# A first modulation in five uneven pieces with its x and value weights loaded piece by piece, and a last 512-column projection done as two halves

## The chip, the cores and the metric

The kernel runs on one core of one Trainium2 chip. The metric is the device time of one execution in microseconds (us); less is better. The kernel before was run three times: 1462.21, 1459.61 and 1459.7 us, median 1459.7 us.

## The reference, cut to what matters

One inference step of two layers (DEPTH = 2) over 384 tokens of width 1024: 128 prompt tokens and 256 sample tokens. Each layer has a mixing part and a feed-forward part (FFN), and each part starts from a modulated input. All data is float32.

```
ada   = silu(c) @ ada_w + ada_b              c: one row for the prompt, one for the sample
shift, scale, ... = split(ada)               each of 1024 columns
h     = x * (1 + scale) + shift              the modulated input (h1 for the mixing part)
mix   = mLSTM(h @ in_w[...]) , conv(...) , retention(h @ in_w[...]) , joined by gates
x     = layer_norm(alpha * x + gate * mix)
h2    = x * (1 + scale2) + shift2
x     = layer_norm(alpha * x + gate2 * (silu(h2 @ w1) * (h2 @ w3)) @ w2)
```

The change touches two places: the first modulation of the first layer with the two value projections that consume it (h @ in_w for the mLSTM values and for the retention values, 512 columns each), and the very last product of the second layer's FFN with its layer norm.

## The kernel before, in words

**Tiles and number format.** The 384 tokens are three token tiles of 128 (t = 0 the prompt, t = 1 and 2 the sample). The width of 1024 is eight feature tiles of 128. A float32 product is made of three matmuls on parts that are rounded to a shorter format: `split` (lines 208 to 210) takes a high part of a weight (`whi`, a cast on ScalarE, line 209) and the rest (`wlo`, a subtraction on VectorE, line 210), and `accum` (lines 255 to 261) issues high by high, high by low, low by high (lines 259, 260, 261). Weights arrive by DMA in tiles `wraw` of 1 MB (three buffers).

**Who sets the order.** A tile scheduler orders each engine's instructions from the program text, dependences and buffers; on an engine they then run in that order. Loads are issued by SyncE (SP) in one queue, strictly in order. A DMA is given one of eight completion semaphores in turn, so an issue also waits until the DMA eight places before it has landed.

**The head, lines 976 to 1074.** x is loaded whole, three DMAs of 512 KB (lines 997, 999), and TensorE turns all of it into feature-major tiles `xT` by 24 transposes (line 1005). The first modulation then goes in four pieces q of two feature tiles each. `ada_load(q)` loads the 2 MB of `ada_w` that give shift and scale for those 256 columns, as four DMAs with rows of 256 numbers (line 988), and two small DMAs of `ada_b` (line 994). `ada_part` multiplies them with silu(c) (16 matmuls of 32x256 in the program, each two in the trace, `adaps`, line 1021) and adds the bias on VectorE (line 1024). `ada_mod` spreads the result over partitions (`modps`, line 1030), copies it (lines 1031, 1032), applies it to `xT` on ScalarE (`hfs`, line 1037) and splits h into `h1h` and `h1l` (VectorE, lines 1039, 1040). Six accumulations `vacc` (two value projections by three token tiles, each one bank of PSUM of 512 columns) take the feature tiles of a piece as they come: 144 matmuls of 512 columns in all. The value weights come as four `wraw` tiles of 1 MB, two in front of piece 1's `ada_w` and two in front of piece 3's (line 215, `load_v`). The table `AORD` says after which accumulation the `ada_part` and `ada_mod` of the next piece stand.

**What follows the head.** On SP: constants (`cc`, line 1077), states and small vectors (lines 1081 to 524), the gate weights `wg` (line 812, 64 KB in very short rows), vectors `vr` (lines 1095, 1098), and then the first two 1 MB tiles of the mixing weights (line 247), called r0 and r1 here: r0 holds feature tiles 0 to 3, r1 feature tiles 4 to 7 of the same 512 output columns. On TensorE: the gate product (line 818, 16 matmuls), then the mixing products (lines 259 to 261, `ps`, 384 columns), which use r0 first and r1 after it, with one gate transposition between (line 542).

**The tail.** `proj` (from line 462) runs the last product: per half hf of 512 output columns and per token tile t, `tokB` accumulates 8 feature tiles per 1024 rows of w2, and `resid` (line 426) scales (line 429, `gmix`), adds to x (line 433) and takes statistics (line 437, `bn`). For hf = 1 `norm` follows: line 442 joins the statistics, line 324 and GpSimd's line 325 make the reciprocal root, lines 450 and 451 apply it to two halves of x, and `put_out` (line 491 to 493) stores them.

## Time and profile before

| | |
|---|---|
| median of three runs | 1459.7 us |
| the profiled execution's own time | 1460.56 us |
| its span in the trace | 1458.8 us |
| TensorE (PE) matmul busy | 1424.8 us, 98% of the span |
| VectorE (DVE) busy | 927.9 us, 64% |
| ScalarE (ACT) busy | 589.0 us, 40% |
| GpSimd (POOL) busy | 64.6 us, 4% |
| moved by DMA | 226.08 MB, 155 GB/s over the span |
| mean granted TensorE clock | 0.993 of full speed |

Times in the trace start at 0 with the span. The timeline view has one row for a run of equal instructions: start, how long the run took from its first start to its last end, engine, line, operation, what is written from what, shapes and count, and in brackets how long the engine was idle before it and what ended that. The profiled execution is 0.86 us above the median of the runs; 1.8 us of its time lie outside the span.

### The profile page before, as it was taken

The page shows a single profiled execution, that of the slowest core. Times are in us where ns is not written, and L with a number is a line of the kernel's source. Part 1 is how long each engine was busy: PE and PEld are TensorE (multiplying, and loading weights), DVE is VectorE, ACT ScalarE, POOL GpSimd, SP SyncE. Part 2 cuts the span into 40 slices and gives each one's busy share as a digit, 9 for nine tenths or more (in the row PEclk, how much of TensorE's full clock was granted, in tenths as well). Part 3 has the DMA queues.
Part 4 walks back from the last instruction along what each step waited for, and adds up shares of the span by engine and source line. Part 5 has one row for each costly group of instructions (what it writes and reads, how often), then busy time and mean ns, then how long its engine had stood idle before and what let it go on. Part 6 is the DMA issues. An engine that isn't in the chain of part 4 may idle for free.

```text
span 1458.8 us, 20429 instructions
## 1 busy us (share of the span) xinstructions
PE 1424.8 (98%) x7990; PEld 1295.3 (89%) x7990; DVE 927.9 (64%) x1845; ACT 589.0 (40%) x1090; POOL 64.6 (4%) x102
## 2 busy tenths in 40 slices
PE   6999999999999999999999999899999999999997
PEld 4799999989988888979977999899999889898996
DVE  3455798987747545354374559879886666544447
ACT  3445458423525323323334365544335254242430
POOL 1000002000100000000000000110000000000000
PEclk8999999999999999999999999999999999999999
DMA  9565255465374474645655332342535526243441
GB/s 316 178 233 177 95 138 172 145 223 182 117 260 159 149 255 138 223 153 177 211 152 162 130 120 66 84 123 88 164 99 170 173 73 203 89 158 100 145 159 43
DMA packets 131712, 226.08 MB, mean 155 GB/s; under 512 B 12552, under 2 KB 62200, under 8 KB 126496
## 3 DMA queue, kind: packets, MB, share of 16 engines
q1 hardware_dynamic: 130144, 222.65, 47.0%
q0 software_dynamic: 1472, 2.14, 0.5%
q8 instruction: 62, 1.02, 0.3%
q14 instruction: 34, 0.28, 0.1%
HBM read 221.05 MB, written 3.71 MB: 154 GB/s over the span
## 4 chain that ended last, share of the span: by engine, by line
PE 83%; DMA 7%; DVE 6%; ACT 2%; issue 1%; POOL 0%; SPq 0%; DVEq 0%; POOLq 0%; ACTq 0%
PE ps L259 25%; PE ps L261 24%; PE ps L260 24%; DMA wraw<-in_in_w_dram 4%; PE adaps L377 3%; DMA adaq<-in_ada_w_dram 1%; DVE wlo L210 1%; DMA wada<-in_ada_w_dram 1%; DVE cacc L783 1%; PE vacc L259 1%; PE vacc L261 1%; PE vacc L260 1%; ACT whi L209 1%; PE adaps L1021 0%; DVE dl L636 0%
## 5 line engine op out<-in xcount | busy, mean ns | idle before, releaser
L209 ACT CAST whi<-wraw 128x512 fp32r<-128x512 f32 (+1 forms) x484 | 337.5, 723 | 593.8 <-PE ps L260 248.3
L210 DVE TENSOR_TENSOR wlo<-wraw,whi 128x512 fp32r<-128x512 f32 (+1 forms) x484 | 383.5, 813 | 215.3 <-PE ps L261 104.1
L259 PE MATMUL ps<-h1h,whi 128*128 128x384 f32 x896 | 306.9, 343 | 3.2 <-ACT whi L209 1.7
L261 PE MATMUL ps<-h1h,wlo 128*128 128x384 f32 x896 | 300.9, 336 | 1.1 <-DVE wlo L210 1.0
L260 PE MATMUL ps<-h1l,whi 128*128 128x384 f32 x896 | 300.2, 335 | 0.0
L259 PE MATMUL ps<-h2h,whi 128*128 128x384 f32 x576 | 193.9, 337 | 0.0
L261 PE MATMUL ps<-h2h,wlo 128*128 128x384 f32 x576 | 192.6, 334 | 0.0
L260 PE MATMUL ps<-h2l,whi 128*128 128x384 f32 x576 | 192.6, 334 | 0.0
L259 PEld LDWEIGHTS ps<-h1h,whi 128*128 128x128 f32 x896 | 168.9, 189 | 18.2 <-ACT whi L209 7.0
L261 PEld LDWEIGHTS ps<-h1h,wlo 128*128 128x128 f32 x896 | 168.6, 188 | 2.2 <-DVE wlo L210 2.0
L260 PEld LDWEIGHTS ps<-h1l,whi 128*128 128x128 f32 x896 | 169.0, 189 | 0.1
L783 DVE SCALAR_TENSOR_TENSOR cacc<-u,cwt,cacc 128x399 f32<-128x399 f32 x232 | 144.3, 627 | 1.9
L259 PEld LDWEIGHTS ps<-h2h,whi 128*128 128x128 f32 x576 | 108.1, 188 | 8.5 <-issue 5.0
L260 PEld LDWEIGHTS ps<-h2l,whi 128*128 128x128 f32 x576 | 108.1, 188 | 0.2
L261 PEld LDWEIGHTS ps<-h2h,wlo 128*128 128x128 f32 x576 | 108.1, 188 | 0.0
L259 PE MATMUL ps<-whi,fAh 128*128 128x512 f32 x264 | 103.4, 392 | 0.0
L261 PE MATMUL ps<-whi,fAl 128*128 128x512 f32 x264 | 102.9, 390 | 0.0
L260 PE MATMUL ps<-wlo,fAh 128*128 128x512 f32 x264 | 102.8, 389 | 0.0
L429 DVE TENSOR_TENSOR gmix<-ps,lnc 128x512 f32<-128x512 f32 x48 | 33.1, 689 | 84.8 <-PE ps L261 84.8
L963 DVE TENSOR_TENSOR gf<-ps,sig 128x384 f32<-128x384 f32 x36 | 20.1, 557 | 84.7 <-PE ps L261 84.7
L259 PEld LDWEIGHTS ps<-whi,fAh 128*128 128x128 f32 x264 | 49.6, 188 | 14.1 <-issue 4.2
L261 PEld LDWEIGHTS ps<-whi,fAl 128*128 128x128 f32 x264 | 49.6, 188 | 10.4
(307 smaller groups left out, 1997.5 us busy)
## 6 DMA issues: line engine op xcount, KB each, us to landing
wraw<-in_in_w_dram SPq DMA_DIRECT2D x64, 1024.0 KB
wada<-in_ada_w_dram SPq DMA_DIRECT2D x40, 1024.0 KB
wraw<-in_ffn_w_dram SPq DMA_DIRECT2D x76, 512.0 KB
wraw<-in_ffn_w_dram SPq DMA_DIRECT2D x28, 1024.0 KB
wraw<-in_out_w_dram SPq DMA_DIRECT2D x8, 1024.0 KB
adaq<-in_ada_w_dram SPq DMA_DIRECT2D x8, 512.0 KB
wraw<-in_mlstm_out_w_dram SPq DMA_DIRECT2D x4, 1024.0 KB
wraw<-in_ret_out_w_dram SPq DMA_DIRECT2D x4, 1024.0 KB
```

Source lines behind the costliest of these rows:

```text
L209: nc.scalar.copy(hi, src)
L210: tt(lo, src, hi.bitcast(F32), op=ALU.subtract)
L259: mm(out, sh, vh, start=(first and i == 0), stop=False)
L260: mm(out, sh, vl, start=False, stop=False)
L261: mm(out, sl, vh, start=False, stop=(last and i == n - 1))
L377: mm(st["ps"][32 * g:32 * g + 32, :], cs[:, k, :], wt[:, 512 * g:512 * g + 512], start=(k == 0), stop=(k == KT - 1))
L429: tt(g, ps, lc[0 if t == 0 else 1, hf], op=ALU.mult)
L783: tc.keep_in_program_order(stt(ac, u[:, k:k + CW], wk, ac, op0=ALU.mult, op1=ALU.add))
L963: tt(f, ps, sg[j], op=ALU.mult)
```

## The change

**Head.** The first modulation goes in five pieces of 1, 2, 2, 2 and 1 feature tiles (`PIECES`). A piece of one tile loads 1 MB of `ada_w` in rows of 128 numbers (512 B) into another buffer, in two DMAs; a piece of two tiles loads as before. x comes in columns: the first 128 columns of the three token tiles through ScalarE's queue, then 256, 256 and 384 columns through SP's, each in front of the piece that needs them, and the transposes are issued one feature tile at a time (`x_turn`) from the table `todo` between the accumulations. The first 512 rows of the two value weights come in three steps each (feature tile 0, tiles 1 and 2, tile 3), the second 512 rows as 1 MB each, and they are split per feature tile (128x512) and not per two (128x1024).

**Tail.** In the last product of the kernel, the last token tile's second 512 columns are accumulated as two halves of 256 columns, one after the other, each with its own `resid`; the statistics of that token tile are taken in groups of 256.

```diff
-AORD = {(0, 0): ((1, 1, 0, 16),), (0, 1): ((0, 1),), (0, 4): ((1, 2, 0, 16),), (0, 5): ((0, 2),),
-        (1, 3): ((1, 3, 0, 16),), (1, 5): ((0, 3),)}
+PIECES = ((0, 1), (1, 2), (3, 2), (5, 2), (7, 1))
...
     def resid(t, hf, ps, lc, first, stats, c=slice(0, 512)):
...
+            if t not in bns:
+                bns[t] = [tmp((P, 4, 6), f"bn{t}", 1), 0]
+            for c0 in range(s.start, s.stop, stats):
+                nc.vector.bn_stats(bns[t][0][:, bns[t][1], :], x[t][:, c0:c0 + stats])
+                bns[t][1] += 1
...
-                ps = tokB(src, wl, t)
+                parts = [slice(0, 512)]
+                stats = 512 if final else 0
+                if final and after is None and t == NT - 1:
+                    stats = 256
+                    if hf == 1:
+                        parts = [slice(0, 256), slice(256, 512)]
+                for c in parts:
+                    ps = tokB(src, [(h[:, c], l_[:, c]) for h, l_ in wl], t)
+                    with urgent() if final and hf == 1 else nullcontext():
+                        resid(t, hf, ps, lc, first, stats, c)
...
+    def load_v(h, k0, k1, which=(0, 1)):
+        for i in which:
+            off = (O_MV, O_RV)[i]
+            if k0 == 0:
+                raws[h, i] = wp.tile([P, 4, 512], F32, tag="wraw", name="wraw", bufs=WRAW)
+            r0 = h * 512 + k0 * P
+            nc.sync.dma_start(raws[h, i][:, k0:k1, :],
+                              inw[r0:r0 + (k1 - k0) * P, off:off + 512].rearrange("(k p) f -> p k f", p=P))
...
+    x_load(nc.scalar, slice(0, P))
+    ada_load(0)
+    xT = []
+    x_turn(0)
+    load_v(0, 0, 1)
+    x_load(nc.sync, slice(P, 3 * P))
+    ada_part(0)
     ada_mod(0)
...
+    ada_load(1)
+    load_v(0, 1, 3)
+    x_load(nc.sync, slice(3 * P, 5 * P))
+    todo = {0: [(1, x_turn, 1), (1, x_turn, 2), (3, ada_part, 1), (4, ada_mod, 1)],
+            1: [(1, x_turn, 3), (1, x_turn, 4), (3, ada_part, 2), (4, ada_mod, 2), (4, v_pre, 3)],
+            2: [(0, x_turn, 5), (0, x_turn, 6), (2, ada_part, 3), (3, ada_mod, 3), (4, x_turn, 7)],
+            3: [(2, ada_part, 4), (3, ada_mod, 4)]}
+    for pi, (f0, nf) in enumerate(PIECES):
+        if pi == 0:
+            ada_load(2)
+            load_v(0, 3, 4)
+            x_load(nc.sync, slice(5 * P, D))
+        elif pi == 1:
+            load_v(1, 0, 4, (0,))
+            ada_load(3)
+        elif pi == 2:
+            load_v(1, 0, 4, (1,))
+            ada_load(4)
...
```

**Where instructions move: SP, the first loads.** Before (x, the first piece, the first value weights, the second piece):

```order
L186 DMA cc<-consts_dram 128x130
L997 DMA x_77<-in_x_prompt_dram 128x1024
L999 DMA x_78<-in_x_sample_dram 128x1024
L999 DMA x_79<-in_x_sample_dram 128x1024
L988 DMA adaq<-in_ada_w_dram 128x6x256
L988 DMA adaq<-in_ada_w_dram 128x2x256
L988 DMA adaq<-in_ada_w_dram 128x4x256 x2
L994 DMA adaq<-in_ada_b_dram 2x256 x2
L215 DMA wraw<-in_in_w_dram 128x4x512 x2
L988 DMA adaq<-in_ada_w_dram 128x6x256
```

Now, from the same first row to the first DMA of the second piece (the first 128 columns of x are on ScalarE's queue and not in these rows):

```order
L185 DMA cc<-consts_dram 128x130
L1013 DMA adaq<-in_ada_w_dram 128x8x128 x2
L1018 DMA mrows<-in_ada_b_dram 2x128 x2
L1071 DMA wraw<-in_in_w_dram 128x512 x2
L990 DMA x_77<-in_x_prompt_dram 128x256
L992 DMA x_78<-in_x_sample_dram 128x256
L992 DMA x_79<-in_x_sample_dram 128x256
L1071 DMA wraw<-in_in_w_dram 128x2x512
L1013 DMA adaq<-in_ada_w_dram 128x6x256
```

The 1 MB of piece 0 now stands in front of everything but the small constants, and less of x and of the value weights stands in front of piece 1. From the constants that follow the last piece on (line 1077 before, 1134 now) SP's rows are the same.

**TensorE, the first mixing products.** Before, from the gate transposition on (`h1h_96` is feature tiles 0 to 3 and so needs r0; `h1h_98` is tiles 4 to 7 and needs r1); twelve matmuls on r0 stand in front of these rows:

```order
L542 MATMUL ps_668<-cc_75,mgT_622 128x16 x3
L259 MATMUL ps_715<-h1h_96,whi_636 128x384
L260 MATMUL ps_715<-h1l_97,whi_636 128x384
L261 MATMUL ps_715<-h1h_96,wlo_637 128x384
L259 MATMUL ps_715<-h1h_96,whi_636 128x384
L259 MATMUL ps_642<-h1h_98,whi_630 128x384
L260 MATMUL ps_642<-h1l_99,whi_630 128x384
```

Now, the last rows ahead of the first one on r1; here thirteen matmuls on r0 and the gate transposition stand in front of the first row:

```order
L260 MATMUL ps_696<-h1h_96,wlo_685 128x384
L260 MATMUL ps_769<-h1h_96,wlo_691 128x384
L258 MATMUL ps_769<-h1h_96,whi_690 128x384
L259 MATMUL ps_769<-h1l_97,whi_690 128x384
L260 MATMUL ps_769<-h1h_96,wlo_691 128x384
L258 MATMUL ps_696<-h1h_98,whi_684 128x384
L259 MATMUL ps_696<-h1l_99,whi_684 128x384
```

The first matmul that needs r1 is the 17th of the mixing products before and the 19th now.

**VectorE, the last token tile.** Before, from the last normalising instruction of t = 1 (`x_78`) on:

```order
L451 SCALAR_TENSOR_TENSOR x_78<-x_78,rs,lnc 128x512 x2
L429 TENSOR_TENSOR gmix<-ps,lnc 128x512
L433 TENSOR_TENSOR x_79<-x_79,gmix 128x512
L437 BN_STATS bn_12944<-x_79 128x6
L442 BN_AGGR mv<-bn_12944 128x2
```

Now:

```order
L453 SCALAR_TENSOR_TENSOR x_78<-x_78,rs,lnc 128x512 x2
L428 TENSOR_TENSOR gmix<-ps,lnc 128x256
L432 TENSOR_TENSOR x_79<-x_79,gmix 128x256
L428 TENSOR_TENSOR gmix<-ps,lnc 128x256
L437 BN_STATS bn_12998<-x_79 128x6
L432 TENSOR_TENSOR x_79<-x_79,gmix 128x256
L437 BN_STATS bn_12998<-x_79 128x6
L444 BN_AGGR mv<-bn_12998 128x2
```

Both halves of the last token tile (`x_79`) stand behind the whole chain of t = 1; three instructions of 512 columns became six of 256.

## Rows read from the trace of the kernel before

**Rows 1.** The page: TensorE's busy time.

```profile
PE 1424.8 (98%) x7990; PEld 1295.3 (89%) x7990; DVE 927.9 (64%) x1845; ACT 589.0 (40%) x1090; POOL 64.6 (4%) x102
```

**Rows 2.** Windows of 10 us: busy per engine, granted clock, DMA share, GB/s.

```profile
10.00:20.00 10.00, 5.34 (x52) 3.51 (x50) 4.08 (x11) 4.07 (x9) 0.52 (x1) 0.91 0.94 348
20.00:30.00 10.00, 8.41 (x44) 4.59 (x44) 5.26 (x5) 3.45 (x4) 0.00 (x0) 0.57 1.05 374
50.00:60.00 10.00, 10.00 (x58) 7.22 (x57) 2.88 (x10) 3.57 (x8) 0.00 (x0) 1.00 0.09 10
```

**Rows 3.** Chain of waits up to 80 us: start, us, what.

```profile
3.90 7.54 DMA adaq<-in_ada_w_dram
11.46 13.39 DMA adaq<-in_ada_w_dram
```

**Rows 4.** Timeline of the head, TensorE.

```profile
14.84 0.64 PE L1021 MATMUL adaps<-adaq,cs 128*32 128x256 f32 x8 [0.68 <-DMA adaq<-in_ada_w_dram]
...
20.56 0.80 PE L259 MATMUL vacc<-whi,h1h 128*128 128x512 f32 x1 [3.15 <-DVE h1l L1040]
...
24.89 1.93 PE L1021 MATMUL adaps<-adaq,cs 128*32 128x256 f32 x16 [0.57 <-DMA adaq<-in_ada_w_dram]
...
29.15 1.07 PE L1021 MATMUL adaps<-adaq,cs 128*32 128x256 f32 x16
```

**Rows 5.** Timeline, TensorE: prices of the head's operations.

```profile
7.06 4.95 PE L1005 MATMUL ps<-cc,x 128*128 128x128 f32 x24 [7.06 <-DMA x<-in_x_prompt_dram]
...
36.29 1.93 PE L1021 MATMUL adaps<-adaq,cs 128*32 128x256 f32 x32
...
39.65 0.95 PE L1030 MATMUL modps<-cc,adaq 128*128 128x2 f32 x8
...
66.14 0.39 PE L259 MATMUL vacc<-whi,h1h 128*128 128x512 f32 x1
...
68.86 0.34 PE L818 MATMUL ps<-h1h,wgr 128*32 128x384 f32 x1
```

**Rows 6.** SP's timeline behind the last piece.

```profile
47.26 1.63 SPq L520 DMA_DIRECT2D m0b<-in_state_mlstm_m_dram  x1
...
58.73 0.27 SPq L1095 DMA_DIRECT2D vr<-in_ln_w_dram  x1
...
71.50 0.27 SPq L1095 DMA_DIRECT2D vr<-in_ln_w_dram  x1
```

**Rows 7.** SP's waits up to 100 us: waited for, us in total, times, longest.

```profile
SPq L1095 <- DMA wg<-in_in_w_dram: 6.1, 1, 6.1
SPq L1095 <- DMA wraw<-in_in_w_dram: 6.0, 2, 4.1
```

**Rows 8.** Timeline, the first mixing products and a cast of their weights.

```profile
69.55 1.15 ACT L209 CAST whi<-wraw 128x512 fp32r<-128x512 f32 x2
...
71.66 0.33 PE L259 MATMUL ps<-h1h,whi 128*128 128x384 f32 x1
...
75.23 0.51 PE L259 MATMUL ps<-h1h,whi 128*128 128x384 f32 x2
```

**Rows 9.** DMA view of 22.8 to 28.2 us.

```profile
DMA packets 2099, 2.08 MB, mean 386 GB/s; under 512 B 66, under 2 KB 2099, under 8 KB 2099
```

**Rows 10.** DMA view of 47.2 to 48 us.

```profile
DMA packets 557, 0.17 MB, mean 208 GB/s; under 512 B 452, under 2 KB 541, under 8 KB 556
```

**Rows 11.** Timeline of the tail.

```profile
1449.00 1.41 DVE L451 SCALAR_TENSOR_TENSOR x<-x,rs,lnc 128x512 f32<-128x512 f32 x2
...
1450.20 0.39 PE L261 MATMUL ps<-whi,fAl 128*128 128x512 f32 x1
1450.62 0.69 DVE L429 TENSOR_TENSOR gmix<-ps,lnc 128x512 f32<-128x512 f32 x1 [0.21 <-PE ps L261]
...
1452.80 0.21 DVE L442 BATCH_NORM_AGGREGATE mv<-bn 128x2 f32<-128x12 f32 x1
```

**Rows 12.** The page, a VectorE group of 384 columns: busy us, mean ns.

```profile
L963 DVE TENSOR_TENSOR gf<-ps,sig 128x384 f32<-128x384 f32 x36 | 20.1, 557 | 84.7 <-PE ps L261 84.7
```

More of the change, by code (lines that the diff above doesn't have):

```diff
@@ L1 @@
-from contextlib import ExitStack
+from contextlib import ExitStack, nullcontext
 import numpy as np
@@ L424, in tile_kernel, with resid @@
     bns = {}
-    def resid(t, hf, ps, lc, first, stats):
-        s = slice(hf * 512, (hf + 1) * 512)
-        g = tmp((P, 512), "gmix")
-        tt(g, ps, lc[0 if t == 0 else 1, hf], op=ALU.mult)
+    def resid(t, hf, ps, lc, first, stats, c=slice(0, 512)):
+        s = slice(hf * 512 + c.start, hf * 512 + c.stop)
+        g = tmp((P, 512), "gmix")[:, c]
+        tt(g, ps[:, 0:c.stop - c.start], lc[0 if t == 0 else 1, hf][:, c], op=ALU.mult)
         if first:
@@ L980, in tile_kernel, with x_load, ada_load, x_turn @@
     v1 = alloc_v()
[L982 to L1002 removed]
+    def x_load(eng, s):
+        eng.dma_start(x[0][:, s], a["x_prompt"][0][:, s])
+        for t in (1, 2):
+            eng.dma_start(x[t][:, s], a["x_sample"][0, (t - 1) * P:t * P, s])
+    def ada_load(i):
+        f0, nf = PIECES[i]
+        w = nf * P
+        if nf == 1:
+            per = 16
+            tiles = [wp.tile([P, 16, P], F32, tag="wada", name="adaq", bufs=WADA)]
+            rows = mrows()[:, 0:256]
+        else:
+            per = 6
+            tiles = [m6((P, 6, 256), name="adaq") for _ in range(3)]
+            rows = tiles[2][:, 4:6, :].rearrange("p a n -> p (a n)")
+            nc.gpsimd.memset(rows, 0.0)
+        for s in range(2):
+            u = 8 * s
+            while u < 8 * s + 8:
+                n = min(8 * s + 8, (u // per + 1) * per) - u
+                k0 = u - 8 * s
+                c0 = s * D + f0 * P
+                nc.sync.dma_start(tiles[u // per][:, u % per:u % per + n, :],
+                                  a["ada_w"][0, k0 * P:(k0 + n) * P, c0:c0 + w].rearrange("(k p) f -> p k f", p=P))
+                u += n
+        for s in range(2):
+            c0 = s * D + f0 * P
+            nc.sync.dma_start(rows[0:2, s * w:(s + 1) * w], a["ada_b"][0, c0:c0 + w].partition_broadcast(2))
+        aq[i] = tiles, rows, per
+    def x_turn(f):
         ps = psum()
@@ new lines, in load_v, with v_split @@
+    def load_v(h, k0, k1, which=(0, 1)):
[6 more added lines that the diff above has]
+                              inw[r0:r0 + (k1 - k0) * P, off:off + 512].rearrange("(k p) f -> p k f", p=P))
+    def v_split(i, k):
+        if k % 2 == 0:
+            whls[i, k // 2] = [wp.tile([P, 2, 512], F32R, tag=tag, name=tag, bufs=n)
+                               for tag, n in (("whi", WHI), ("wlo", WLO))]
+        hi, lo = (v[:, k % 2, :] for v in whls[i, k // 2])
+        if (i, k) not in done:
+            done.add((i, k))
+            split(hi, lo, raws[k // 4, i][:, k % 4, :])
+        return hi, lo
@@ new lines, in v_pre @@
+    def v_pre(k):
+        for i in range(2):
+            v_split(i, k)
+    x_load(nc.scalar, slice(0, P))
[5 more added lines that the diff above has]
+    ada_part(0)
+    ada_mod(0)
+    ada_load(1)
[5 more added lines that the diff above has]
+            3: [(2, ada_part, 4), (3, ada_mod, 4)]}
@@ L1059, in tile_kernel @@
+    for pi, (f0, nf) in enumerate(PIECES):
[9 more added lines that the diff above has]
+            ada_load(4)
         n = 0
+        ws = {}
         for i in range(2):
-            k0 = (2 * q) % 4
-            hi, lo = whl([P, 2, 512], raws[q // 2, i][:, k0:k0 + 2, :])
+            ws[i] = [v_split(i, k) for k in range(f0, f0 + nf)]
@@ L1063, in tile_kernel @@
             for t in range(NT):
-                if q == 0:
+                if pi == 0:
                     vacc[i, t] = psum("vacc")
-                accum(vacc[i, t], [(ha.part(2 * q + k, slice(t * P, (t + 1) * P)), (hi[:, k, :], lo[:, k, :]))
-                                   for k in range(2)], q == 0, q == 3)
-                for fn, *args in AORD.get((q, n), ()):
-                    (ada_part if fn else ada_mod)(*args)
+                accum(vacc[i, t], [(ha.part(f0 + k, slice(t * P, (t + 1) * P)), ws[i][k]) for k in range(nf)],
+                      f0 == 0, f0 + nf == KT)
@@ L1070, in tile_kernel @@
+                for at, fn, arg in todo.get(pi, ()):
+                    if at == n:
+                        fn(arg)
                 n += 1
```

78 lines of the change are left out of this document (21 added, 57 removed).

## The prediction

> **What bounds the kernel now.** The page comes first: TensorE's matmuls are busy for 1424.8 us, 98% of the span [rows 1]. Apart from the two ends the kernel is a queue of matmuls, so the 34 us or so that are left over are the only thing that a change of order can win, and they lie at the head and at the tail. The windows of 10 us show how the head spends them: from 10 to 20 us TensorE is busy for 5.34 us, from 20 to 30 us for 8.41 us but at a granted clock of 0.57, so mostly at 1.2 GHz [rows 2]. The chain of waits says what releases it: DMA waits of 7.54 and 13.39 us for `ada_w`, one behind the other, up to 24.9 us [rows 3]. The timeline gives the steps: the last part of the first piece has landed at 14.84 us, the first value product starts at 20.56, the second piece's part at 24.89, and from 29.15 us on TensorE runs without a wait [rows 4] until the gate product at 68.86 [rows 5], which is 39.7 us of dense work.
>
> Behind that, SP's queue matters. The last piece of `ada_w` has landed by 47.26 us, when SP gets past the waits on it. Then come states, `wg`, for which SP waits 6.1 us until 58.73, and the first mixing weights; r1 has landed by 71.50, at the end of a wait of 4.1 us [rows 6, 7]. So 24.2 us lie between the last piece and r1, in which the DMA engines move only 10 GB/s from 50 to 60 us [rows 2]: a chain of latencies, and one that does not depend on TensorE. Now it is just in time: the second of the two matmuls that start at 75.23 us is the first on r1 [rows 8].
>
> **The change, the head on TensorE.** Before, 3.67 MB (x 1.57, first piece 2.10) must land until 14.84. Now 1.25 MB do (0.20 of x, 1.05 of `ada_w`). The 2.42 MB left out are 6.3 us at the 386 GB/s of a stretch of `ada_w` alone [rows 9], so piece 0 is there at about 8.5 us. From landing to the first value product took 5.7 us [rows 4]. With one feature tile the bias, the scaling and the splits are half as long, and I take 4.5 (3.5 to 5.7): first value product at 13 us instead of 20.56.
>
> But a piece of one tile feeds only 18 of the 144 matmuls, and then piece 1 is awaited. Ahead of its end stand 4.79 MB (x 0.59, `ada_w` 3.15, value weights 1.05), which is 1.12 MB more than lay ahead of 14.84 us: 2.9 us, and 0.5 for the shorter rows, so 18.2, and its products start at about 23. Still to do then, at full clock: 126 matmuls of 512 columns at 0.227 ((68.86 - 66.14)/12) [rows 5], 28.6; `adaps` of pieces 2 to 4 at 1.93, 1.93 and half of it, 4.8; `modps` 0.95, 0.95 and half, 2.4; 15 transposes. Those cost at most 4.95/24 = 0.21 each, which holds waits for x, and at least the 0.12 of a `modps` matmul, which is a weight load and hardly more [rows 5]; I take 0.13, nearer to the latter, 2.0. That is 37.8 us. To it come waits between pieces, 1.4 (0 to 3), and what the slow clock still takes after 23 us, 1.5 (0 to 3), because in the trace it came back only at about 28. The value products end at 63.7 (61 to 68) instead of 68.86. **TensorE alone would gain 4.9 us.**
>
> Smaller edits of the head go together. Splitting value weights per feature tile makes casts and subtractions of 512 columns out of those of 1024: eight more of each on ScalarE and VectorE, which are busy 4.07 and 4.08 us of 10 to 20 and 3.45 and 5.26 us of 20 to 30 [rows 2]. The work hides beside the loads; without that cover it costs a few tenths. SP issues eleven more DMAs before the mixing weights, each half a microsecond or so in a queue that waits for landings anyway.
>
> **The head on the transfers.** Up to the last piece the same 14.2 MB must land, and then the same chain of SP follows. So r1 cannot come earlier than 24.2 us after the last piece, whatever TensorE does. When does the last piece land? The stream starts some 0.5 us earlier, since no whole x is issued ahead. Against that, 2.1 MB of `ada_w` now come in rows of 512 B. The trace has no long stretch of such rows: `ada_w` in rows of 1 KB ran at 386 GB/s [rows 9], a stretch in which 452 of 557 packets were below 512 B at 208 [rows 10]. That is 5.4 or 10.1 us for the 2.1 MB, a loss of 0 to 4.7. I take 1.1, nearer to the first, because most of the second stretch's packets are far smaller; and 0.3 for x in shorter rows. The dips of the stream could also fill up in another order, so earlier by 1.5 is possible. Last piece: 0.9 us later than before (1.5 earlier to 4.5 later).
>
> A rule can be weighed here. The Trainium skill (page "DMA: Bandwidth & Descriptors", section "Specifications") puts the smallest transfer for full rate at 512 B. By that rule the rows of 512 B would cost nothing and the last piece would land 0.2 us earlier than before; no row here shows such rows alone.
>
> What does r1 allow? Landed at about 71.3 in the old timing, and cast in 0.6 (1.15 for two [rows 8]), it can be used at 71.9. Its first matmul stood at 75.4 [rows 8]. In the new order two more matmuls on r0 lie ahead of it, 0.35 us, which are work done earlier. So the chain allows 75.4 + 0.35 - 71.9 = 3.85 us, less the 0.9 by which it comes later: 2.95. **The head gains the smaller of 4.9 and 2.95, so 2.9 us**, and TensorE waits for r1 for the rest. Behind r1 the weights are loaded as buffers come free, which TensorE's pace sets, so the gain should last to the end.
>
> **The tail.** Before, VectorE finishes t = 1 at 1450.41, TensorE ends just behind, and VectorE starts on the last tile at 1450.62; three instructions of 512 columns take it to the joining of statistics at 1452.80 [rows 11], 0.727 apart. In the new order all six instructions of 256 columns stand behind the whole chain of t = 1, so that a first half that is ready earlier cannot be used before 1450.41. One of 512 columns takes 0.69 [rows 11], one of 384 takes 0.557 [rows 12]: 0.133 for 128 columns, so 0.42 for 256, and 0.46 apart. Six are 2.76 against 2.18, started 0.17 sooner: **0.4 us slower** (between -0.1, if half the columns took half the time, and 0.6). On TensorE 48 matmuls of 256 columns replace 24 of 512. None with weights as wide is in the trace at 256 columns; a `modps` matmul, with a weight load of the same size and 2 columns, takes 0.12 [rows 5], and half of 0.227 is 0.11, so 0.12, 5.8 us in place of 5.4. The second half then ends at 1451.0, before VectorE comes to it at 1451.4. No gain from a full-width price either way: the upper bound is 0.227 each, a rival below.
>
> **The sum.** -2.9 + 0.4 = -2.5 us. The profiled execution took 1460.56 us, 1458.8 of it in the span; on it this makes 1458.1. It stood 0.9 above the median of the three runs, and on the median of 1459.7 the forecast is **1457.2 us**. A difference of 0.2%, 2.9 us, is about what a measurement of this kernel can tell from none; the forecast lies just inside.
>
> **Rivals.**
> *The transfers do not bind.* If rows of 512 B run like those of 1 KB, or the smaller loads close the dips, r1 is in time and more of TensorE's 4.9 us are kept: -4.9 + 0.4, 1455.2 (1453.3 to 1456.6). For it: the stream moved 348 GB/s from 10 to 20 us against 386 at its best [rows 2, 9], so there is something to fill. Against it: every byte is still needed and the chain behind is untouched. By the rule of the Trainium skill named above ("DMA: Bandwidth & Descriptors"), the chain would allow 4.05 us, and 1456.0 would come out, which belongs here.
> *The transfers eat it all.* If the last piece lands 3.5 us or more later, r1 comes when it came before: 0 + 0.4, 1460.1 (1459 to 1461.5). For it: more and shorter transfers in a queue with eight semaphores. Against it: issue was not what the chain showed.
> *The slow clock stays, slower.* In the trace the sparse matmuls of 10 to 20 us were followed by a clock of 0.57 [rows 2]. The change makes the sparse part longer: 18 matmuls at 13 us, then a wait, then piece 1. At 1.2 GHz a matmul of 512 columns costs 0.2 us more. If the 36 of piece 1 all ran so, that is 7.2 us, which outweighs the 4.9 and leaves +2.3 + 0.4, 1462.4. It decides from 25 such matmuls on. Against it: from about 23 us on work is dense, and the trace got its clock back in such work. The Trainium skill ("TensorE: Matmul & The Clock Gate", section on oscillation) says that waits for DMA between bursts of matmuls make each burst start at the low clock; the row of 20 to 30 us agrees, and by this rule piece 0's products and the start of piece 1's would run at half speed.
> *The halves cost full price.* If a matmul of 256 columns took 0.227, the second half would end at 1456.1, and the tail would lengthen by 4.3 us more: 1461.5. Against it stands the 0.12 of `modps`.
>
> **How the numbers follow.** Forecast 0.53 (its own range 1455.8 to 1459.0), transfers free 0.20, all eaten 0.14, slow clock 0.09, full price 0.04. Faster by over 0.2%, below 1456.8: all of the second and two fifths of the forecast's case, 0.41. Slower, above 1462.6: the last two, whose centres lie just below that bound, taken whole because nothing else stands for this side, 0.13. The rest is 0.46. A range of 1454.0 to 1460.8 leaves out the two slow cases and the outer edges of two others, about 0.2.
>
> **What would show it.** In the profile after: first value product at about 13 us and first one of piece 1 at about 23; gate product at 63 to 65 instead of 68.86; the first matmul on r1 waiting for ScalarE's cast, and that for the DMA, at about 72.8; SP past the last piece at about 48. In the tail, statistics joined 2.8 us after t = 1 ends, with TensorE already done. I am wrong if TensorE runs from the gate product into r1 without a wait, if the clock is below 0.9 after 30 us, or if the last matmul ends more than 3.5 us earlier than it did.

## The result, and the profile after

The changed kernel took 1468.84 us, the median of six runs (1467.51 to 1470.02); the kernel before took 1459.72 in six runs beside it (1459.61 to 1462.21). The ratio is 1.0061 (95% interval 1.005 to 1.0071): 9 us slower, where 2.5 us faster was forecast. The profiled execution took 1469.12 us, 1467.3 of it in the span, so the spans differ by 8.5 us; those 8.5 us are what the traces have to explain.

TensorE's part of the page, which answers to [rows 1]:

```profile
PE 1429.3 (97%) x8046; PEld 1299.2 (89%) x8046; DVE 929.1 (63%) x1860; ACT 589.9 (40%) x1098; POOL 65.1 (4%) x103
```

TensorE is busy 4.5 us longer, so half of the loss is idle time and half is work that ran slower or was added. The windows of 10 us, which answer to [rows 2] (the span of the window, then PE, PEld, DVE, ACT, POOL busy with counts, the granted clock, the DMA share and GB/s):

```profile
10.00:20.00 10.00, 7.73 (x39) 5.84 (x40) 4.64 (x9) 3.02 (x6) 1.91 (x4) 1.00 0.85 311
20.00:30.00 10.00, 8.98 (x51) 6.38 (x50) 3.89 (x9) 3.39 (x8) 0.00 (x0) 0.83 1.01 364
30.00:40.00 10.00, 10.00 (x73) 7.33 (x72) 4.03 (x10) 3.57 (x7) 0.00 (x0) 1.00 0.76 248
50.00:60.00 10.00, 8.16 (x25) 6.29 (x24) 5.43 (x11) 7.06 (x15) 0.00 (x0) 0.66 0.38 95
```

From 10 to 30 us TensorE does better than before. But the transfers slow down to 248 GB/s from 30 to 40 us, and from 50 to 60 us, where TensorE had run without a gap at full clock, it is busy for 8.16 us at a granted clock of 0.66. TensorE's timeline shows the places; it answers to [rows 4, 5, 8]:

```profile
13.28 0.79 PE L258 MATMUL vacc<-whi,h1h 128*128 128x512 f32 x1 [2.24 <-DVE h1h L1060]
...
18.69 1.07 PE L1042 MATMUL adaps<-adaq,cs 128*32 128x256 f32 x16
...
20.59 1.07 PE L1042 MATMUL adaps<-adaq,cs 128*32 128x256 f32 x16
...
25.40 0.79 PE L258 MATMUL vacc<-whi,h1h 128*128 128x512 f32 x1
...
48.74 1.05 PE L1051 MATMUL modps<-cc,adaq 128*128 128x2 f32 x8 [0.86 <-DVE adaq L1044]
...
52.02 0.79 PE L258 MATMUL vacc<-whi,h1h 128*128 128x512 f32 x1 [1.84 <-DVE h1h L1060]
...
70.97 0.34 PE L825 MATMUL ps<-h1h,wgr 128*32 128x384 f32 x1
...
76.62 0.45 PE L258 MATMUL ps<-h1h,whi 128*128 128x384 f32 x1 [2.70 <-ACT whi L208]
...
92.03 0.83 PE L569 MATMUL ps<-cc,GG 128*128 128x128 f32 x6
```

The first value product comes at 13.28 us, 7.3 earlier than before. Then the lead melts. Piece 1's first product comes at 25.40, and not because TensorE stood waiting for piece 1's weights: from 13.28 to 21.66 us it has no idle time, and both halves of piece 1's `adaps`, at 18.69 and 20.59, start without a wait. Piece 0's first six products, 0.43 apart, six transposes and nine more products stand in front of them. Piece 3 waits twice (0.86 and 1.84 us), and from 52.02 to 57.73 its matmuls stand 0.43 apart where those at full clock stand 0.23 apart, so at 1.2 GHz; the gate product, 68.86 before, is at 70.97. Behind it a wait of 2.70 us that was not there at all: the first mixing product, 71.66 before, is at 76.62, and waits not for r1 but for r0. A fixed point behind both weight tiles is the product on `GG`. In TensorE's timeline of the kernel before it is this row:

```profile
85.36 0.83 PE L562 MATMUL ps<-cc,GG 128*128 128x128 f32 x6
```

So the head has lost 92.03 - 85.36 = 6.7 us there: 2.1 at the gate product, 2.9 more at the first mixing product, which waits for r0, and 1.7 more behind it. The last part is no wait for r1; TensorE has none between 76.62 and 92.03. From 78.58 to 81.75 some ten matmuls of 384 columns stand 0.32 apart in place of 0.17, which is 1.5 us, and the window says why (columns as above):

```profile
78.50:81.80 3.30, 3.30 (x13) 3.30 (x12) 2.95 (x12) 1.89 (x5) 0.00 (x0) 0.51 0.25 84
```

The granted clock is 0.51, where the kernel before had 1.00 from 70 us on. So the wait of 2.70 us was followed, 2 us after its end, by a slow stretch. Of the remaining 1.8 us one half is a longer wait at 308 us (2.5 us for a tile of `ada_w` of the next modulation where it was 1.6), and the other lies in the second layer; the tail adds nothing.

Why is r0 late? The chain of waits ahead of the first mixing product says it (start, us, what):

```profile
63.88 0.35 PE modps L1051 x4
64.33 0.10 POOL mrows L358
...
64.79 0.23 POOL vr L1148
...
67.03 1.37 DMA vr<-in_ln_b_dram
...
68.48 7.45 DMA wraw<-in_in_w_dram
...
75.95 0.63 ACT whi L208
```

SP's timeline, which answers to [rows 6], and its longest wait up to 100 us, which answers to [rows 7]:

```profile
53.31 0.42 SPq L819 DMA_DIRECT2D wg<-in_in_w_dram  x1
65.05 0.25 SPq L1152 DMA_DIRECT2D vr<-in_mlstm_norm_w_dram  x1
...
68.48 0.94 SPq L246 DMA_DIRECT2D wraw<-in_in_w_dram  x2
```

```profile
SPq L1152 <- POOL vr L1148: 11.5, 1, 11.5
```

And GpSimd's timeline at 64 us:

```profile
64.33 0.53 POOL L358 MEMSET mrows<- 128x512 f32 x1 [51.31 <-PE modps L1051]
```

Read from the bottom up: the pieces of one feature tile put their rows into `mrows`, and there is only one such buffer. Its next user is the modulation that fills the gaps later in the layer; it must clear the buffer, and can do so only when piece 4's `modps` matmuls have read it, at 64.23 us. Piece 4 comes last, so GpSimd stands for 51.31 us. In its queue behind that clearing stand the clearings of the vector tiles `vr`; SP may not load a `vr` before that, and behind the `vr` in SP's queue stand r0 and r1. In the kernel before, the same clearing of `mrows` ran at 0.82 us, since nobody else used the buffer, and that of `vr` at 34.84.

The transfers, too, came later. The gate weights' DMA `wg` is issued at 53.31, where SP's timeline before had

```profile
49.42 0.42 SPq L812 DMA_DIRECT2D wg<-in_in_w_dram  x1
...
59.74 0.94 SPq L247 DMA_DIRECT2D wraw<-in_in_w_dram  x2
```

so SP stood 3.9 us behind there already. The slack of the stream opened from 10 to 15 us, where it moved 233 GB/s (390 before), and from 29 to 34 us. The DMA view of the second stretch after, and the one before:

```profile
DMA packets 531, 0.95 MB, mean 189 GB/s; under 512 B 32, under 2 KB 179, under 8 KB 531
```

```profile
DMA packets 1362, 1.68 MB, mean 336 GB/s; under 512 B 46, under 2 KB 1050, under 8 KB 1361
```

Last, the tail. VectorE's timeline, which answers to [rows 11]:

```profile
1457.53 1.41 DVE L453 SCALAR_TENSOR_TENSOR x<-x,rs,lnc 128x512 f32<-128x512 f32 x2
1458.85 0.42 DVE L428 TENSOR_TENSOR gmix<-ps,lnc 128x256 f32<-128x256 f32 x1
...
1461.22 0.26 DVE L444 BATCH_NORM_AGGREGATE mv<-bn 128x2 f32<-128x24 f32 x1
```

From the end of t = 1 (1457.53 + 1.41 = 1458.94) to the joining it takes 2.28 us, where it took 2.39 before. On TensorE the matmuls of 256 columns start 0.12 us apart, as these two neighbours show, and the last ends at 1459.42, before VectorE wants the second half at 1459.64:

```profile
1459.02 0.28 PE L259 MATMUL ps<-wlo,fAh 128*128 128x256 f32 x1
1459.14 0.28 PE L260 MATMUL ps<-whi,fAl 128*128 128x256 f32 x1
```

### The profile page after: what moved, and what is told of

It is laid out like the page before. It is cut to its first block, busy times and chain, and to the rows that moved or that the text cites. A ratio compares the mean times of both kernels' runs of the same rounds, so it can differ in the third digit from the quotient of the medians.

```text
span 1467.3 us, 20584 instructions
## 1 busy us (share of the span) xinstructions
PE 1429.3 (97%) x8046; PEld 1299.2 (89%) x8046; DVE 929.1 (63%) x1860; ACT 589.9 (40%) x1098; POOL 65.1 (4%) x103
## 4 chain that ended last, share of the span: by engine, by line
PE 82%; DVE 8%; DMA 6%; ACT 1%; issue 1%; POOL 1%; SPq 0%; DVEq 0%; POOLq 0%; ACTq 0%
PE ps L258 24%; PE ps L260 24%; PE ps L259 24%; DMA wraw<-in_in_w_dram 5%; PE adaps L376 3%; DVE wlo L209 2%; DVE cacc L790 1%; DMA wada<-in_ada_w_dram 1%; PE vacc L258 1%; PE vacc L259 1%; PE vacc L260 1%; PE adaps L1042 1%; ACT whi L208 1%; POOL hrs L324 0%; PE svo L674 0%
## 5 line engine op out<-in xcount | busy, mean ns | idle before, releaser
L258 PE MATMUL ps<-whi,fAh 128*128 128x512 f32 (+1 forms) x272 | 104.8, 385 | 0.0
L260 PE MATMUL ps<-whi,fAl 128*128 128x512 f32 (+1 forms) x272 | 104.3, 383 | 0.0
L259 PE MATMUL ps<-wlo,fAh 128*128 128x512 f32 (+1 forms) x272 | 104.2, 383 | 0.0
L428 DVE TENSOR_TENSOR gmix<-ps,lnc 128x512 f32<-128x512 f32 (+1 forms) x49 | 33.2, 678 | 83.5 <-PE ps L260 83.5
```

Of the source, the lines that this page charges most:

```text
L258: mm(out, sh, vh, start=(first and i == 0), stop=False)
L259: mm(out, sh, vl, start=False, stop=False)
L260: mm(out, sl, vh, start=False, stop=(last and i == n - 1))
L428: tt(g, ps[:, 0:c.stop - c.start], lc[0 if t == 0 else 1, hf][:, c], op=ALU.mult)
```

## The experiments

Two theories stood against each other. **The queue:** r0 and r1 are late because the single `mrows` buffer stops GpSimd and through it SP. **TensorE and the transfers:** even without that the new head is slower, by the late last piece, the late value weights and the clock. All ratios are to the kernel before on the same chip, whose medians were 1460.75, 1461.11, 1461.05 and 1460.78 us in the four groups of runs.

**Head or tail.** The kernel before with the new tail alone (the functions `tokB`, `resid`, `norm` and `proj` of the change):

> The kernel before with the new tail alone. Theory from the profile of the changed kernel: its tail took as long as the old one (statistics joined 8.42 us later than before at a shift of 8.53 in front of it), so -0.1 to 0, within 0.5 us of 1459.7. The prediction's sum had +0.4. Rival (the halves are the loss): +2 us or more.

1460.74 us, ratio 0.9999 (0.999 to 1.0008). The change with the old tail:

```diff
                 if final and after is None and t == NT - 1:
-                    stats = 256
-                    if hf == 1:
-                        parts = [slice(0, 256), slice(256, 512)]
+                    stats = 512
```

> The changed kernel with the old tail (one product of 512 columns, statistics of 512). If the whole loss is the head's, the total is that of the changed kernel within 0.6 us, 1468.2 to 1469.5; if the tail had a part in it, it falls by that part.

1471.05 us, ratio 1.0067 (1.0053 to 1.0081). The tail is neutral, and the whole loss is the head's.

**A buffer of its own for the rows of the small pieces**, so that GpSimd's queue goes through:

```diff
-            rows = mrows()[:, 0:256]
+            rows = tmp((P, 512), "gmix")[:, 0:256]
+            nc.gpsimd.memset(rows, 0.0)
```

> The changed kernel, but the two pieces of one feature tile keep their rows in a buffer of their own (the idle buffer of gmix) instead of the single buffer mrows. Theory (GpSimd's queue): in the changed kernel the next clearing of mrows waits until the modps of the last piece has read it (64.3 us), the clearing of vr stands behind it on GpSimd, SP's vr loads wait for that 11.5 us, and the mixing weights r0 and r1 stand behind those on SP. With a buffer of its own SP is held by wg only, r0 is issued at about 63 instead of 68.5 and lands at about 70, TensorE no longer waits for its cast and the first mixing product starts at about 73.9 (changed kernel 76.6, before 71.7). Total 1461.5 to 1464.5, that is 4 to 7 us below the changed kernel and 2 to 4.5 above the one before. Rival (the transfers are late by themselves): r0 still lands at 74 or later and the total stays within 1.5 us of 1468.8.

1466.59 us, ratio 1.0039 (1.0027 to 1.0052), so 0.0022 or 3.2 us less than the change, less than was expected; the two intervals leave some 2 us of doubt on either side. SP's timeline and one of its waits in this kernel:

```profile
53.48 0.42 SPq L819 DMA_DIRECT2D wg<-in_in_w_dram  x1
...
63.88 0.94 SPq L246 DMA_DIRECT2D wraw<-in_in_w_dram  x2
```

```profile
SPq L1153 <- DMA wg<-in_in_w_dram: 6.3, 1, 6.3
```

The wait for GpSimd is gone, and the old chain is back, with the old wait for `wg` (6.3 us; 6.1 in [rows 7]). But all of it stands 4.1 us later than before, from `wg` (53.48 against 49.42) to r0 and r1 (63.88 against 59.74). That is the chain that the prediction reckoned with, and the later last piece in it. The product on `GG` is 4.6 us late.

**The vectors behind the weights.** The same queue from the other side: the `vr` loads are put behind r0 and r1 on SP.

```diff
-    spawn(vectors())
+    spawn(vectors(), 2)
```

> The changed kernel (one buffer mrows as there), with the loads of the small vectors vr put behind the first two mixing weight tiles r0 and r1 on SP, by starting their step two ticks later. If what stands ahead of r0 on SP is the loss behind the value products, r0 and r1 are issued at about 54 and 60 us and land before 72, TensorE goes from the gate product into the mixing products without a wait at 73.9 us, 2.2 later than before, and the total is 2 to 4 us above the kernel before of this call. What is left is then TensorE's own lateness in the head. Rival (the rest of the loss is not in this queue): more than 5 us above.

1465.29 us, ratio 1.0024 (1.0013 to 1.0034). Against the change's 1.0061 that is 0.0037, 5.4 us, again with some 2 us of doubt: what the queue cost, GpSimd's stop and the old chain's own lateness together. SP's timeline and TensorE's:

```profile
54.41 4.85 SPq L246 DMA_DIRECT2D wraw<-in_in_w_dram  x2
```

```profile
54.44 0.80 PE L258 MATMUL vacc<-whi,h1h 128*128 128x512 f32 x1 [1.84 <-DVE h1h L1060]
...
72.09 0.34 PE L825 MATMUL ps<-h1h,wgr 128*32 128x384 f32 x1
...
74.88 0.33 PE L258 MATMUL ps<-h1h,whi 128*128 128x384 f32 x1
...
88.33 2.62 PE L569 MATMUL ps<-cc,GG 128*128 128x128 f32 x22
```

r0 is asked for at 54.41 and r1 less than 4.9 us later, and TensorE goes from the gate product into the mixing products without a wait. What is left of the head's loss, 88.33 - 85.36 = 3.0 us, is TensorE's own: its gate product is at 72.09. Both theories are right, then: 5.4 us the queue, 3 to 4 us the rest, each to within some 2 us.

**The clock of piece 3**, on top of this: thirteen matmuls of 384 columns whose result nobody reads keep TensorE at work while piece 3's modulation is made, 4 before its `modps` and 9 after.

```diff
         pm = psum("modps")
+        def warm(n):
+            for _ in range(n if i == 3 else 0):
+                mm(pm[:, P:P + T], ha.part(0, slice(0, P))[0], ha.part(1)[0], start=True, stop=True)
+        warm(WARM[0])
...
+        warm(WARM[1])
```

> As the run with vr behind, and 13 matmuls of 384 columns that nobody reads fill TensorE's wait for the fourth piece (from 47.9 to 52 us). If the low clock that follows that wait (matmuls of 512 columns 0.43 apart from 52 to 57.7 us) comes from the idle stretch, the clock stays at 1.00 there, the value products end 2.4 us earlier, at about 68.6, and the total is 1.5 to 2.5 us below the run with vr behind. Rival (the clock falls all the same, or the fill delays the chain): no more than 0.5 us below it, or above.

1464.19 us, ratio 1.0027 (1.0017 to 1.0037), not told apart from the kernel without them. The window of 50 to 60 us, and TensorE's timeline:

```profile
50.00:60.00 10.00, 8.42 (x49) 6.63 (x42) 5.23 (x12) 5.46 (x12) 0.00 (x0) 1.00 0.44 120
```

```profile
55.45 0.96 PE L259 MATMUL vacc<-whi,h1h 128*128 128x512 f32 x3 [1.08 <-ACT whi L209]
...
71.60 0.34 PE L826 MATMUL ps<-h1h,wgr 128*32 128x384 f32 x1
```

The clock is kept (1.00; 0.83 without), but the piece's first value product waits for ScalarE's cast of the value weights and comes at 55.45 instead of 54.44; the gate product gains 0.5 us. The low clock was not the limit by itself: behind it stand the casts. ScalarE's timeline shows what these wait for:

```profile
54.40 0.48 ACT L1031 COPY xT<-ps 128x384 f32<-128x384 f32 x1 [11.58 <-PE ps L1026]
54.78 0.62 ACT L209 CAST whi<-wraw 128x512 fp32r<-128x512 f32 x1
```

It is no landing. ScalarE runs in order, and the copy of the last transposes of x stands ahead of the casts; for it ScalarE was idle for 11.58 us (9.11 in the change, whose casts follow at 52.35 without a wait). No run moved that copy, so what it is worth stays open.

**The second value tile earlier.** The other way to read the late casts is that the second value tile is late. Its buffer comes free when the last rows of the first tiles are split. The split is put ahead of piece 2's `ada_part`:

```diff
-            1: [(1, x_turn, 3), (1, x_turn, 4), (3, ada_part, 2), (4, ada_mod, 2), (4, v_pre, 3)],
+            1: [(1, x_turn, 3), (1, x_turn, 4), (3, v_pre, 3), (3, ada_part, 2), (4, ada_mod, 2)],
```

> As the run with vr behind, and the split of the value weights of feature tile 3 stands ahead of the third piece's bias add in the program. In the changed kernel VectorE idled 6.4 us in front of that bias add with the split behind it, so that the buffer for the last 1 MB of value weights came free at 37 us only. Theory: those weights are issued at about 32 and land by 43, their casts and the nine products of feature tile 4 stand ready when the fourth piece is awaited, the wait and the low clock at 50 to 57 us go, value products end at 67 to 69, and the total is 2 to 4 us below the run with vr behind, 0 to 1.5 above the kernel before. Rival (order alone decides little, the fourth piece's landing is what is late): within 1 us of the run with vr behind.

1464.35 us, ratio 1.002 (1.001 to 1.0029), not told apart from the vectors behind the weights alone (1.0024). The tile is issued at 36.48 instead of 37.06, not at 32: SP's queue reaches it no sooner. Two kernels ask for it further ahead in the queue, in front of piece 3's `ada_w`, the first with rows of its own as above, the second on top of the earlier split:

```diff
         elif pi == 1:
-            load_v(1, 0, 4, (0,))
+            load_v(1, 0, 4)
             ada_load(3)
         elif pi == 2:
-            load_v(1, 0, 4, (1,))
             ada_load(4)
```

> As the first of these runs (rows in a buffer of their own), and the second half of the retention value weights is loaded in front of the fourth piece (before ada_load(3)) instead of behind it. Theory: in the changed kernel TensorE ran dry at 46.4 to 52 us because those weights landed only at 46.7, so that nine products of feature tile 4 could not cover the chain from the fourth piece's landing to its h; the clock then fell to half for 5 us. With the weights there, the value products end at 66.5 to 69 instead of 71.0, r1 then binds (lands at about 74 to 75), and the total is 1459 to 1462. Rival (the piece's own chain is what TensorE waits for): the wait at about 50 us stays, value products end at 70.5 or later, total as in the first run.

> As the run before it, and all value weights of the second half are loaded ahead of the fourth piece. In the earlier try of this order SP stood 7.3 us in front of the last value weights for a buffer, which held the fourth piece back. With the buffer free at about 32 SP should pass, the fourth piece comes about 2 us later than in the run before it, and the total is within 1.5 us of that run. If SP stands again for more than 4 us, it is 2 to 4 us slower.

1470.77 us, ratio 1.0063 (1.0047 to 1.0079), and 1468.33 us, ratio 1.0045 (1.0031 to 1.0059): both worse than without (1.0039 and 1.002). SP's longest wait in the first, up to 60 us:

```profile
SPq L1072 <- DVE wlo L209: 7.3, 1, 7.3
```

In the second it is 5.1 us. SP stands for the buffer, and piece 3's `ada_w` stands behind it. In these two ScalarE does wait for that tile, 5.6 and 5.7 us, and TensorE behind ScalarE 3.4 and 3.5 us, around 45 to 48 us. In neither place was the tile early: with three buffers, SP stood for one.

**Is it the number of DMAs?** The other way to read the dip of 29 to 34 us is that SP waits for landings, since each of more and smaller DMAs takes one of eight semaphores. One bias DMA per piece in place of two, and x in three steps in place of four, on top of the earlier split:

```diff
-        for s in range(2):
-            c0 = s * D + f0 * P
-            nc.sync.dma_start(rows[0:2, s * w:(s + 1) * w], a["ada_b"][0, c0:c0 + w].partition_broadcast(2))
+        nc.sync.dma_start(rows[0:2, 0:2 * w].rearrange("p (s w) -> p s w", s=2),
+                          a["ada_b"][0, 0:2 * D].rearrange("(s d) -> s d", s=2)[:, f0 * P:f0 * P + w].partition_broadcast(2))
...
-    x_load(nc.sync, slice(3 * P, 5 * P))
+    x_load(nc.sync, slice(3 * P, D))
...
-            x_load(nc.sync, slice(5 * P, D))
```

> As the run with the early split (third of the previous call), with fewer and larger transfers: the two loads of ada_b of a piece are one, and x comes in three steps instead of four (128, 256 and 640 columns). Theory: with eight semaphores in turn, an issue waits for the landing of the one eight places before, and where most of the eight are small the stream runs dry; in the changed kernel 10 to 15 us moved 233 GB/s and 29 to 34 us 189 GB/s (before: 379 from 8 to 12 and 314 from 30 to 35). With fewer small ones 29 to 34 us move over 300 GB/s, the last piece lands at 46 to 48 instead of 49.7, and the total is 1 to 2 us below the run with the early split. Rival (SP stands for buffers, not for semaphores): the second dip stays below 230 GB/s and the total is within 0.7 us of that run.

1469.82 us, ratio 1.005 (1.0033 to 1.0067), slower than the earlier split alone (1.002). A window and SP's longest wait up to 60 us:

```profile
20.00:30.00 10.00, 8.19 (x56) 5.44 (x56) 3.89 (x9) 2.89 (x6) 0.00 (x0) 0.83 1.07 394
```

```profile
SPq L1070 <- DVE wlo L209: 5.9, 1, 5.9
```

The stream is faster up to 30 us (394 GB/s), and what it gains it loses behind, standing for a buffer: the dip moves from landings to buffers. From 40 to 50 us it moves 192 GB/s. The same with the thirteen unread matmuls:

> As the run before it, with the 13 unread matmuls in TensorE's wait for the fourth piece. Where that wait and the low clock behind it are still there, 1 to 2.5 us below the run before it; where casts on ScalarE bind behind the wait, as in the first run with such a fill (0.5 us earlier at the gate product), within 0.7 us.

1465.69 us, ratio 1.0031 (1.0021 to 1.0041). Here the product on `GG` is at 85.86, only 0.5 us later than before, and the kernel is still 4.6 us slower, 4.2 in the spans. So in this kernel nearly all of the loss lies behind the head. Its wait at 308 us is 2.3 us (1.6 before), and behind that wait ten matmuls of 384 columns stand 0.32 apart, at a granted clock of 0.57 (1.00 before):

```profile
310.00:314.00 4.00, 4.00 (x20) 3.52 (x13) 1.41 (x3) 0.45 (x1) 0.00 (x0) 0.57 0.75 240
```

That is 0.7 us of wait and 1.5 of clock. Some 1.1 us more arise in the second layer and were not traced to a cause.

**Can the kernel before gain from a kept clock?** Two kernels put 30 unread transposes beside the first `modps`, the first into the bank of PSUM that `modps` uses, the second into one of their own; the edit is the second's.

```diff
+        def warm(n, late=False):
+            for j in range(n):
+                src = rows[:, (j % 4) * P:(j % 4) * P + P] if late else xT[0][:, j % 4, 0:P]
+                tr(pw[:, P * (j % 3):P * (j % 3) + P], src, ident)
+        if q == 0:
+            pw = psum("warm")
+            warm(WARM[0])
...
+        if q == 0:
+            warm(WARM[1], True)
```

> The kernel before, and 30 transposes of 128x128 that nobody reads fill TensorE's waits between the first piece's parts and up to the first value product (13 to 20.5 us). Theory: the clock of 0.50 from 18.6 to 28.3 us comes from the idle stretches in front of it; kept busy, TensorE runs the first 12 value products 0.23 apart instead of 0.43, is ahead by 2 to 2.7 us at 29 us, the value products end that much before 68.9, r1 is still in time (it had 3.5 us in hand), and the total is 1.5 to 2.7 us below the kernel before. Rival (that stretch waits for transfers and splits whatever the clock): within 0.7 us of the kernel before.

> The kernel before with unread transposes as fill once more, now in a PSUM bank of their own, so that the copies of modps do not wait for them (in the first try they did: the first value product came at 22.0 instead of 20.6 us and the second piece's loads were late behind it). 6 fill the waits between the first piece's parts, 24 the wait behind modps. Theory (the low clock of 18.6 to 28.3 us comes from idle stretches and costs the value products of the first piece 0.2 us each): the clock stays at 1.00 to 24 us or longer, first value product no later than 20.8, value products end 1.5 to 2.5 us before 68.9, total 1 to 2.5 us below the kernel before. Rival (that stretch waits for transfers and splits whatever the clock): gate product within 0.7 us of 68.9, total within 0.7 us.

1466.44 us, ratio 1.0029 (1.0018 to 1.0041), and 1460.76 us, ratio 1.0001 (0.9992 to 1.001). In the first the copies of `modps` on VectorE had to wait for the transposes in their bank, and the first value product came at 22.02 instead of 20.56. The second is shown by two windows and TensorE's timeline:

```profile
20.00:30.00 10.00, 8.05 (x64) 5.29 (x62) 6.16 (x7) 3.69 (x4) 0.00 (x0) 0.96 1.07 378
30.00:40.00 10.00, 10.00 (x66) 7.31 (x65) 3.08 (x7) 1.86 (x4) 1.17 (x4) 0.83 0.88 320
```

```profile
17.51 4.42 PE L1034 MATMUL warm<-cc,adaq 128*128 128x128 f32 x24
...
31.11 0.63 PE L260 MATMUL vacc<-whi,h1h 128*128 128x512 f32 x1
...
68.78 0.34 PE L819 MATMUL ps<-h1h,wgr 128*32 128x384 f32 x1
```

From 20 to 30 us the granted clock is 0.96 where it was 0.57 [rows 2]. But the 24 transposes themselves ran at half speed: from 18 to 20 us the granted clock is 0.50 with TensorE busy throughout, and the first value product comes at 21.69, 1.1 later than before. And from 31 us on, with TensorE at work without a gap, it falls to 1.2 GHz for eight matmuls, and the gate product is at 68.78 instead of 68.86. The slow stretch moved and did not go; whether another fill than transposes would have held the clock there, no run says. No kernel of the twelve was faster than the one before.

## Why the prediction was wrong

**Right: the first landing, the first value product** (13 forecast, 13.28), from the bytes ahead (landing at 8.5 forecast; the wait for the last part ends at 8.34) and the chain behind them (4.5 forecast, 4.9). **Right: the tail**, forecast at +0.4, bounds -0.1 to 0.6: it came out at -0.1, because instructions of 256 columns at 0.42 us each start 0.33 to 0.47 apart, not 0.46 throughout, and the first of them starts 0.3 us sooner, not 0.17. Its price on TensorE, 0.12 for 256 columns, was the forecast's, and so the rival of the full price falls. **Right: rows of 512 B cost little.** In the 5 to 8 us window, where nearly all packets were of that kind, the DMA view gives

```profile
DMA packets 1879, 1.04 MB, mean 347 GB/s; under 512 B 36, under 2 KB 1815, under 8 KB 1879
```

which is near the 386 of [rows 9] and far from the 208 of [rows 10]: for 2.1 MB 0.6 us, where the sum had 1.1. The Trainium skill (page "DMA: Bandwidth & Descriptors", section "Specifications") has full rate from 512 B on; the row comes near it without reaching it.

**Wrong, and the largest part that was measured: "and then the same chain of SP follows".** This was taken from the rows of SP being the same in the order. The rows were the same; what they wait for was not. The change moves the rows of two pieces into `mrows`, a single buffer with another user, and GpSimd's queue was not followed behind that user, though `mrows` stood among the change's first loads. The wait of 11.5 us took the place of the one for `wg` (6.1), and put r0's issue at 68.48 instead of some 60.6 (59.74 before, and 0.9 later as forecast). The buffer alone is worth 3.2 us (rows of their own), the queue with the old chain's own lateness 5.4 (vectors behind the weights). A part of that is clock: the wait for r0 brought a slow stretch behind it. Of the rivals none had this wait. The chain itself was read rightly: with the buffer out of the way it came back step for step, 4.1 us later.

**Wrong by size: the last piece.** Forecast 0.9 us later (1.5 earlier to 4.5 later). SP's step behind it, the issue of `wg`, is 3.9 us later with the queue's stop still ahead. That lies inside the bounds but on the side of the rival "the transfers eat it all", against which the text said that issue was not what the chain showed. The dips of 10 to 15 and of 29 to 34 us were the price: SP in order, waiting for landings, and, once these were fewer, for a buffer (5.9 us). The added issues had been put at nothing; there are twelve (43 in place of 31), not eleven. With eight fewer the stream was faster up to 30 us, but the kernel was no faster. The dips did not fill up in the new order; they moved.

**Wrong by sign: "TensorE alone would gain 4.9 us".** It lost 2.1, seven more (the forecast's own 63.7 in place of 68.86 is 5.2, which makes it 7.3). Three terms of that sum make up most of it. Piece 1's products started at 25.40 and not 23: 2.4. The step that failed there is "and then piece 1 is awaited": TensorE never stood for it, and its own work of piece 0, a part of it at half speed, was what came last. The waits between pieces were 0.86 + 1.84 = 2.7 and not 1.4: 1.3. The slow clock after 23 us was put at 1.5 because it had come back once in dense work; but piece 3's gap brought a second slow stretch, from 52.02 to 57.73, some thirteen matmuls at 0.2 us more each, beside some five or six at 25 us: close to 4 us, some 2.3 more than the term. Together about 6 of the 7; the last one was not followed term by term. So the rival of the slow clock had the mechanism, but set it at piece 1, where the sparse work is; it struck at piece 3, behind waits of 0.86 and 1.84 us for its own h, with nothing else ready because the casts of the second value tile came only at 52.35, and again at 78.58, behind the wait for r0. And it was no independent price: with the clock kept, the gate product gained 0.5 us only, since the casts came next.

**Of the signs named for being wrong**, that the clock is below 0.9 after 30 us was the one that came (0.66 from 50 to 60 us).

**Open.** That "the gain should last to the end" was not so for a loss either: some 2 us of the change's loss, and 3 to 4 us in the kernels whose head was nearly mended, arise behind the head, at 308 us (waits of 1.0 to 3.2 us in different versions, 1.6 before, in some with a slow stretch behind them) and in the second layer. No experiment separated them. Nor is a trace exact to less than 2 us: with the tail alone changed the head is the same, and yet its product on `GG` comes 1.65 us earlier than before:

```profile
83.71 1.05 PE L570 MATMUL ps<-cc,GG 128*128 128x128 f32 x8
```

So the divisions of the loss that are read from one trace against another are known to no better than that, and the runs of one kernel spread over 2.2 to 7.0 us, which makes a loss of 2 us hard to divide (those of the kernel before spread over 6.0 us in the first group).

## What to carry to other kernels

When a change borrows a buffer that already has a user, find that user's next claim on it, and follow what stands behind that claim on its engine's in-order queue, and behind those in the DMA queue: here a clearing of 0.53 us stopped two queues and cost some 3 of the 9 us. Smaller first pieces brought the start forward here by 7 us, but not the last bytes, which came some 4 us later, and a lead at the start is only worth what the next late input leaves of it. A chain of waits in the trace of before shows what binds there and not what will bind next, so it can't speak against a rival about a queue that the change makes longer.

## What the runs showed of the hardware that was not expected

A granted clock held up by unread matmuls is no gain by itself. Beside piece 3 it went from 0.83 to 1.00 in its window and gave 0.5 us at the gate product; beside the first piece of the kernel before, it was 0.50 while the fill itself ran, rose from 0.57 to 0.96 in the window behind, and then fell to 1.2 GHz some ten us later in the middle of dense work, so that nothing was won. Nor does a wait alone tell what follows: at 308 us the clock fell behind waits of 2.3, 2.9 and 3.1 us in three versions, and stayed at 1.00 behind 2.5 us in the change and 2.3 with the tail alone. And the record of the clock can miss a slow stretch: the first six value products of the change stand 0.43 apart, as at 1.2 GHz, while the granted clock from 13.2 to 16 us reads 1.00. The Trainium skill ("TensorE: Matmul & The Clock Gate", section "HAM oscillation — how this bites in real kernels") ties the low clock to waits for DMA between bursts of matmuls. The stretch at 78.58 us agrees with it in part: it follows a wait at whose end of the chain stands a DMA, but begins 2 us after it. The one at 52 us follows waits that VectorE ended, and the one at 31 us, with no wait ahead of it for over a microsecond, is not explained by it.

VectorE's instructions of 256 columns take 0.42 us each in the trace, but the six of the tail span 2.37 us from the first start to the joining, 0.395 a piece. They start at 1458.85, 1459.30, 1459.64, 1459.98, 1460.31 and 1460.75, and the joining at 1461.22. Where an instruction reads what the one just before it wrote (the second, the sixth and the joining) it starts 0.44 to 0.47 after it; where two neighbours belong to different halves, 0.33 to 0.34. The forecast's 0.46 was the price of the first kind: in the kernel before all three were of it, and the halves of the change let others in between.
